# A PEER expert layer with 64 of 384 dense tokens moved to gathered rows, on one Trainium2 core

## The chip, the core and the metric

The kernel runs on one NeuronCore of a Trainium2 chip. TensorE (PE; its weight loads are shown as PEld), VectorE (DVE), ScalarE (ACT) and GpSimd (POOL) each work through a list of instructions in order and wait for each other on semaphores; SyncE (SP) and POOL issue the transfers between the core's memory (SBUF) and the device memory (DRAM), which 16 DMA engines carry out. The metric is the device time of one execution in microseconds (us), lower being better.

## The reference

512 tokens of width 1024 pass through one block: a modulated norm, a retention branch and a spatial gating branch, a residual, a second norm, and a PEER layer over 16,384 experts, each with one row of `expert_u` and one of `expert_v`. The change touches only the PEER layer:

```python
q = (hb @ w_q).reshape(T, PEER_HEADS, 2, PEER_HALF)
s = jnp.einsum('thpc,hpnc->thpn', q, sub_keys)
sub_s, sub_i = lax.top_k(s, K)                      # K = 16, 8 heads
...
expert = k1 * PEER_N_KEYS + k2                      # 8 x 16 = 128 experts for each token
g = jax.nn.softmax(top_s.astype(jnp.float32), axis=-1).astype(hb.dtype)
ue = expert_u[expert]
act = jax.nn.gelu(jnp.einsum('td,thkd->thk', hb, ue), approximate=False) * g
ve = expert_v[expert]
return jnp.einsum('thk,thkd->td', act, ve)
```

Behind it stand the second residual (`x + gate2 * peer`) and a final RMS norm.

## The kernel before

The first 500 us compute the two branches and the residual, and are not touched. The PEER layer handles its 512 tokens in two ways.

**Dense tokens** (`TA` = 384, token tiles 0 to 2, 128 tokens each) meet all 16,384 experts, in 128 chunks of 128 experts. For a chunk, `u_mm` multiplies a unit of `uT` (512 KB) with the normed tokens: 24 matmuls of 384 columns. Each float32 product is three passes over float32r parts: high by high, high by low, low by high. GELU follows, then a multiplication with a dense table of softmax weights (zero where a token has not chosen the expert); `a_make` does this (`aw` at L1235, rounded to `ah` at L1237, rest `al` at L1240). `v_mm` then takes each tile's 128 columns of `ah` or `al` as weights and a unit of `v` (its parts `wh`, `wl`) as the moving operand: 3 tiles x 3 passes x 2 halves of 512 columns, 18 matmuls for each chunk, all at L1252.

**Gathered tokens** (tile 3, 128 tokens, one on each partition) fetch only the rows they chose. `gather` (L1132) has POOL issue an indirect DMA of 128 rows of 4 KB, `consume` has DVE read it: a dot product with `h2B` (L1142) for a row of `u`, a weighted sum into `accB` (L1147) for a row of `v`. That makes 128 + 128 = 256 gathers.

The order is written out by hand. `plan()` sets the steps between the second norm and the main loop: the product keys and top-16 searches (`st1`, `st2`), the lists, the one-hot blocks (`oh`, then `wmm` on TensorE) which build the dense weight table, and beside them `U` steps, chunks of `u_mm` done ahead of the main loop, with their results written to DRAM (`sd`, L876, from `spl`). The planner adds 4.05 to its clock `P` for a `U` step and a cost to its clock `V` for each DVE step, lets DVE steps in while `V` is at most `P` + 6, and grants `GPU` = 0.75 `gather` steps for each `U`. It yields 78 `U` steps, 24 one-hot blocks of 16 tokens and 48 `gather` steps; 51 gathers are consumed before the main loop with the 3 left in their buffers. A finished pair of one-hot blocks goes to DRAM as 2 MB on POOL's queue (`wd`, L1118). In the one-hot part the gathers have three buffers, in the main loop eight.

The main loop (from L1371) runs over the 128 chunks; the last four are done tile by tile at the end. An iteration does `u_mm` two chunks ahead if that chunk was not done ahead of the loop, `v_mm`, the loads of `sd` and `wd` pieces on SP's queue, and `a_make`, with some `consume` and `gather` pairs put between `ah` and `al`; their number is spread evenly by `cost` and `per`. Units of `uT` and `v` come through `Stream`: a load on SP's queue five units ahead, a rounding on ACT to `wh` (L76), a subtraction on DVE to `wl` (L79).

After the loop `res` and `fin` (or `res_half`, `fin_half` for the last tile) add the residual and the final norm for one tile while TensorE does the next.

Of the kernel before, what the change touches and what calls it, by code (L numbers as in the profile page):

```python
# [17 lines left out]
OP = mybir.AluOpType  # L18
# [9 lines left out]
TA = 384  # L28
NA = TA // 128
# [6 lines left out]
GPU = 0.75  # L36
# [142 lines left out]
def block_kernel(ctx: ExitStack, tc: tile.TileContext, a, out, dbg=None):  # L179
# [28 lines left out]
    def rsqrt(p, dst, src, n, mul, tag):  # L208
        """dst = 1/sqrt(src*mul + EPS) with one Newton step."""
# [14 lines left out]
    # big and wt stay to the end; tmp serves the first half  # L224
# [23 lines left out]
    def ada_dma(k, where=None, eng=None):  # L248
        """unit k = [128 k, 8 kc, 256 cols] in two halves"""
# [6 lines left out]
    def ada_acc(k):  # L256
        """weighted sum over the k chunks, in two chains"""
# [14 lines left out]
    def ada_sum(acc, which, d, gcol):  # L272
        """shift and scale columns of channel chunk d; the gain is folded into the scale."""
# [98 lines left out]
    # x in, rms statistics; TensorE is kept busy meanwhile, for its clock  # L372
# [50 lines left out]
    # first pass: four token tiles of the first group and two of the second, by chunks of the contraction  # L423
    # as the modulation comes in
# [94 lines left out]
    # layer norm of the gated values  # L519
# [16 lines left out]
    # q, k with rotary, transposed to [dk, head, t]  # L536
# [28 lines left out]
    # spatial gating  # L565
# [47 lines left out]
    # gate b and the gated branch b, transposed  # L613
# [17 lines left out]
    # retention: P_h[j, i] = (k_j . q_i) * decay, unrolled over the key chunks  # L631
# [59 lines left out]
    # output gate of the retention branch, transposed with the group-norm gain  # L691
# [125 lines left out]
    def h2_split(t):  # L817
# [6 lines left out]
        if t == NA:  # L824
            for q in range(2):
# [3 lines left out]
                A.copy(h2B[:, q * 512:(q + 1) * 512], ps)  # L829
# [28 lines left out]
    def u_mm(parts=((0, TA),)):  # L858
# [619 lines left out]
```

## Time and profile before

| | us |
|---|---|
| median of 3 runs | 1778.95 (1775.25 to 1779.43) |
| span of the profiled execution | 1776.7 |
| TensorE busy in it | 1746.2 (98%) |
| VectorE busy | 1344.6 (76%) |
| ScalarE busy | 785.3 (44%) |
| GpSimd busy | 436.0 (25%) |

The profile is one execution; its span, first to last instruction, lies 2.3 us under the median of the runs. "Busy" of TensorE counts pipelined matmuls whose ends are modelled, so the distance between the starts of two matmuls tells more than the length of one. A "DMA share" is the mean busy share of the 16 DMA engines, and GB/s what they moved. The granted clock of TensorE is 1.0 at 2.4 GHz and 0.5 at 1.2 GHz.

### The profile page before, as it was taken

How to read it: one execution, taken by the hardware profiler on the slowest of the kernel's cores; microseconds unless marked ns; L12 is line 12 of the kernel's file. 1: busy time of each engine (PE TensorE's matmuls, PEld its weight loads, DVE VectorE, ACT ScalarE, POOL GpSimd, SP SyncE). 2: the span in 40 equal slices, each digit the busy share in tenths (PEclk: the TensorE clock that was granted, in tenths of full speed). 3: DMA queues.
4: the chain of work that ended last, by engine and by line, in shares of the span. 5: the costliest groups of instructions: out<-in, count | busy, mean ns of one | idle time of the engine just before them, and what ended most of it. 6: DMA issues, size and time to landing. Idle time of an engine off the chain costs nothing.

```text
span 1776.7 us, 24625 instructions
## 1 busy us (share of the span) xinstructions
PE 1746.2 (98%) x9117; PEld 1529.8 (86%) x9117; DVE 1344.6 (76%) x2618; ACT 785.3 (44%) x1051; POOL 436.0 (25%) x369
## 2 busy tenths in 40 slices
PE   9999999999999989999999999999999999999997
PEld 7888888888888889999999978888888888888885
DVE  7677762442754999999999767877778878878787
ACT  6532521333362344468999633333333333333334
POOL 0000100000010003233334233433434333434422
PEclk9999999999999999999999999999999999999998
DMA  9634742123433237777999999998989898989973
GB/s 379 228 106 147 260 178 83 60 95 107 143 119 116 72 102 268 267 250 242 337 329 331 341 380 342 339 339 323 333 324 348 326 338 331 342 306 356 338 274 132
DMA packets 119913, 445.47 MB, mean 251 GB/s; under 512 B 13360, under 2 KB 13360, under 8 KB 119664
## 3 DMA queue, kind: packets, MB, share of 16 engines
q1 hardware_dynamic: 67392, 246.61, 37.4%
q0 software_dynamic: 52400, 197.29, 31.8%
q8 instruction: 71, 1.16, 0.2%
q14 instruction: 50, 0.41, 0.1%
HBM read 399.15 MB, written 44.70 MB: 250 GB/s over the span
## 4 chain that ended last, share of the span: by engine, by line
PE 81%; DVE 10%; issue 4%; DMA 2%; POOL 1%; ACT 1%; SPq 0%; POOLq 0%; ACTq 0%; DVEq 0%
PE acc L1252 30%; PE mm L867 7%; PE mm L865 7%; PE mm L866 7%; PE mm L356 4%; PE mm L358 4%; PE mm L357 4%; PE mm L354 4%; PE mm L352 4%; PE mm L353 4%; DVE wl L79 2%; PE mm L1113 1%; PE mm L1114 1%; POOL gw L1132 1%; PE mm L668 1%
## 5 line engine op out<-in xcount | busy, mean ns | idle before, releaser
L79 DVE TENSOR_TENSOR wl<-raw,wh 128x1024 fp32r<-128x1024 f32 x356 | 436.0, 1228 | 257.7 <-ACT wh L76 256.9
L76 ACT CAST wh<-raw 128x1024 fp32r<-128x1024 f32 x356 | 373.2, 1052 | 84.4 <-PE mm L354 38.3
L867 PE MATMUL mm<-h2H,wl 128*128 128x384 f32 (+1 forms) x1032 | 346.9, 336 | 8.3 <-DVE wl L79 8.3
L865 PE MATMUL mm<-h2H,wh 128*128 128x384 f32 (+1 forms) x1032 | 348.3, 337 | 1.4 <-ACT wh L76 1.4
L866 PE MATMUL mm<-h2L,wh 128*128 128x384 f32 (+1 forms) x1032 | 345.5, 335 | 0.0
L1252 PE MATMUL acc<-wh,ah 128*128 128x512 f32 x768 | 244.4, 399 | 5.6 <-ACT ah L1237 5.6
L1252 PE MATMUL acc<-wl,ah 128*128 128x512 f32 x768 | 244.3, 399 | 0.0
L1252 PE MATMUL acc<-wh,al 128*128 128x512 f32 x768 | 244.0, 398 | 0.0
L1132 POOL DMA_INDIRECT gr<-in_v_dram,eidx x128 | 174.9, 1366 | 266.0 <-DVE wqb L1147 232.8
L1237 ACT CAST ah<-aw 128x384 fp32r<-128x384 f32 x128 | 65.8, 514 | 321.7 <-DVE aw L1235 321.7
L867 PEld LDWEIGHTS mm<-h2H,wl 128*128 128x128 f32 x1032 | 195.0, 189 | 11.4 <-DVE wl L79 11.3
L865 PEld LDWEIGHTS mm<-h2H,wh 128*128 128x128 f32 x1032 | 195.2, 189 | 4.2 <-ACT wh L76 2.0
L866 PEld LDWEIGHTS mm<-h2L,wh 128*128 128x128 f32 x1032 | 195.0, 189 | 1.9
L1252 PEld LDWEIGHTS acc<-wh,ah 128*128 128x128 f32 x768 | 145.0, 190 | 37.5 <-ACT ah L1237 6.4
L1252 PEld LDWEIGHTS acc<-wh,al 128*128 128x128 f32 x768 | 145.5, 189 | 35.8
L1252 PEld LDWEIGHTS acc<-wl,ah 128*128 128x128 f32 x768 | 145.5, 189 | 35.3
L1147 DVE SCALAR_TENSOR_TENSOR wqb<-gr,cB,wqb 128x1024 f32<-128x1024 f32 x128 | 164.1, 1282 | 1.9
L1132 POOL DMA_INDIRECT gr<-in_u_dram,eidx x77 | 99.5, 1292 | 160.1 <-DVE gr L1142 138.7
L352 PE MATMUL mm<-wh,hH 128*128 128x512 f32 x256 | 101.8, 398 | 0.0
L1132 POOL DMA_INDIRECT gw<-in_u_dram,eidx x51 | 75.5, 1480 | 102.0 <-DVE gw L1142 94.0
L354 PE MATMUL mm<-wh,hL 128*128 128x512 f32 x256 | 100.1, 391 | 0.2
L353 PE MATMUL mm<-wl,hH 128*128 128x512 f32 x256 | 99.8, 390 | 0.0
(292 smaller groups left out, 2745.9 us busy)
## 6 DMA issues: line engine op xcount, KB each, us to landing
raw<-in_uT_dram SPq DMA_DIRECT2D x128, 512.0 KB, 6.4
raw<-in_v_dram SPq DMA_DIRECT2D x128, 512.0 KB, 6.5
raw<-in_w_in_dram SPq DMA_DIRECT2D x60, 512.0 KB, 4.0
wqb<-wd SPq DMA_DIRECT2D x33, 768.0 KB, 9.3
wd<-stg POOLq DMA_DIRECT2D x12, 2048.0 KB, 12.5
sd<-spl POOLq DMA_DIRECT2D x39, 384.0 KB, 6.1
sp<-sd SPq DMA_DIRECT2D x39, 384.0 KB, 7.2
ada<-in_w_ada_dram POOLq DMA_DIRECT2D x28, 512.0 KB, 4.6
```

The lines of the kernel that those rows point to most:

```text
L76: self.nc.scalar.copy(h, r)
L79: self.nc.vector.tensor_tensor(l, r, h.bitcast(F32), op=OP.subtract)
L352: T.matmul(ps, sH[:, d, ab], wH[:, dd, :], start=st, stop=False)
L353: T.matmul(ps, sH[:, d, ab], wL[:, dd, :], start=False, stop=False)
L354: T.matmul(ps, sL[:, d, ab], wH[:, dd, :], start=False, stop=sp)
L356: T.matmul(ps, wH[:, dd, ab], sH[:, d, :], start=st, stop=False)
L865: T.matmul(ps[:, p:q], h[:, d, :], h2H[:, d, p:q], start=(d == 0), stop=False)
L866: T.matmul(ps[:, p:q], h[:, d, :], h2L[:, d, p:q], start=False, stop=False)
L867: T.matmul(ps[:, p:q], l[:, d, :], h2H[:, d, p:q], start=False, stop=(d == ND - 1))
L1132: P.indirect_dma_start(out=r, out_offset=None, in_=a["u"] if i < NJ else a["v"], in_offset=bass.IndirectOffsetOnAxis(ap=E_IDX[:, j:j + 1], ...
L1147: V.scalar_tensor_tensor(accB, r, cB[:, j:j + 1], accB, op0=OP.mult, op1=OP.add)
L1252: T.matmul(accs[2 * t + e], x[:, ts], y[:, e * 512:(e + 1) * 512], start=s0, stop=s1)
```

## The change

Half of tile 0 leaves the dense tokens: `TA` = 320. Its first 64 tokens (`HC` = 64) join the gathered ones. Each has 128 experts; the first 64 of them sit on partitions 0 to 63 and the other 64 on partitions 64 to 127 (`EC_IDX`, `gC`), so a gather again fills 128 partitions, and there are 64 + 64 = 128 more gathers of 512 KB. The two half sums are added at the end (`half_b`, `half_a`, `half_res`). Tile 0 has 64 dense tokens left; their 64 high and 64 low parts lie side by side in one tile (`hl`, from column `TA`), so one set of 128 weights carries both, and `v_mm` needs two passes instead of three for that tile: 16 matmuls for a chunk. The sum of the high and the low half comes out on different partitions and is added at the end too. `u_mm` and the table work on 320 columns, the one-hot blocks number 20. The planner's constants change, so its table does.

```diff
-TA = 384
-NA = TA // 128
+NA = 3
+TP = 128 * NA
+HC = 64
+TA = TP - HC
-GPU = 0.75
+GPU = 1.0
@@ plan
-        t["P"] += 4.05
+        t["P"] += 3.5
@@ u_mm
+                cs = slice(HC + p, HC + q)
+                T.matmul(ps[:, p:q], h[:, d, :], h2H[:, d, cs], start=(d == 0), stop=False)
...
@@ h2_split
-        if t == NA:
+        if t in (0, NA):
...
+                    P.dma_start(h2d[:, q * 512:(q + 1) * 512], hc[:HC, :])
@@ lists
+        if t == 0:
+            V.scalar_tensor_tensor(kc, kk[t][0][:HC], 128.0, kk[t][1][:HC], op0=OP.mult, op1=OP.add)
+            V.tensor_copy(ec, kc)
+            A.copy(EC_IDX[:HC, :], ec[:, :HJ])
+            P.dma_start(EC_IDX[HC:, :], ec[:, HJ:])
+            A.copy(gC[:HC, :], gA[:HC, 0:HJ])
+            P.dma_start(gC[HC:, :], gA[:HC, HJ:NJ])
@@ gather, consume
+    NGT = 2 * NJ + 2 * HJ
+    def seg(i):
+        if i < 2 * NJ:
+            return ("u", "v")[i // NJ], i % NJ, E_IDX, (h2B, dots, gB, accB, NJ)
+        i -= 2 * NJ
+        return ("u", "v")[i // HJ], i % HJ, EC_IDX, (h2C, dotC, gC, accC, HJ)
@@ a_make
-        h = mn.tile([128, TA], F32R, name="ah", tag="ah", bufs=4)
-        l = mn.tile([128, TA], F32R, name="al", tag="al", bufs=4)
+        hl = mn.tile([128, 2 * TA + HC], F32R, name="ah", tag="ah", bufs=4)
+        h, l = hl[:, 0:TA], hl[:, TA + HC:]
         A.copy(h, w)
+        A.copy(hl[:, TA:TA + HC], w[:, 0:HC])
@@ v_mm
+            if t == 0:
+                x = hl[:, TA:TA + 128]
+                runs = ((x, vh, st, False), (x, vl, False, sp))
+            else:
+                o = HC + (t - 1) * 128
+                h, l = hl[:, o:o + 128], hl[:, TA + HC + o:TA + HC + o + 128]
+                runs = ((h, vh, st, False), (h, vl, False, False), (l, vh, False, sp))
@@ the end
+    def half_b():
+        part = gr[1][:, 0:2, :]
+        P.dma_start(part[:HC, 1, :], accC[HC:, :])
+    def half_a():
+        for e in range(2):
+            A.copy(part[:, 0, HV[e]], accs[e])
+        nc.sync.dma_start(part[HC:, 1, :], part[:HC, 0, :])
+        A.copy(part[:HC, 0, :], accC[:HC, :])
+    def half_res():
+        V.tensor_tensor(part[:, 0, :], part[:, 0, :], part[:, 1, :], op=OP.add)
+        V.tensor_tensor(part[:, 0, :], part[:, 0, :], gates[:, 1, :], op=OP.mult)
+        V.tensor_tensor(x3[:, 0, :], x3[:, 0, :], part[:, 0, :], op=OP.add)
+        sq(0, slice(0, D), ss3[:, 0:1])
+        V.tensor_tensor(fo[:, 0, :], x3[:, 0, :], fo[:, NA, :], op=OP.mult)
+    half_b()
     for t in range(NA - 1):
         for i, vhl, hl in fin_l:
             v_mm(i, (t,), vhl, hl)
+        if t == 0:
+            half_a()
+            continue
         res(t)
         fin(t)
+        half_res()
+        fin(0)
```

What the planner's table becomes: 122 `U` steps instead of 78, 20 one-hot blocks instead of 24, 106 `gather` steps instead of 48 (55 ahead of the one-hot part, where 22 stood, and 51 in it, where 26 stood); with the last three buffers 109 gathers are consumed before the main loop, 275 remain for it. Of the chunks in the main loop 6 still do their `u_mm` there (50 before), four of these ahead of its first iteration.

TensorE, one chunk of the main loop, from its first matmul on (`acc` are the six banks, two for each token tile; `wh`, `wl` the unit of `v`). Before:

```order
L1252 MATMUL acc_9541<-wh,ah 128x512
L1252 MATMUL acc_9542<-wh,ah 128x512
L1252 MATMUL acc_9541<-wl,ah 128x512
L1252 MATMUL acc_9542<-wl,ah 128x512
L1252 MATMUL acc_9541<-wh,al 128x512
L1252 MATMUL acc_9542<-wh,al 128x512
L1252 MATMUL acc_9543<-wh,ah 128x512
```

And of the change (`ah` now holds both parts):

```order
L1299 MATMUL acc_10951<-wh,ah 128x512
L1299 MATMUL acc_10952<-wh,ah 128x512
L1299 MATMUL acc_10951<-wl,ah 128x512
L1299 MATMUL acc_10952<-wl,ah 128x512
L1299 MATMUL acc_10953<-wh,ah 128x512
```

The two matmuls with the low part as weights are gone for the first tile; the other two tiles keep six each.

VectorE in the main loop, two iterations in the middle (`wqb<-gr,cB,wqb` is a `consume` of a row of `v` into `accB`). Before:

```order
L1235 TENSOR_TENSOR aw<-sp_11932,wqb 128x384
L1147 SCALAR_TENSOR_TENSOR wqb<-gr,cB,wqb 128x1024
L1240 TENSOR_TENSOR al<-aw,ah 128x384
L79 TENSOR_TENSOR wl<-raw,wh 128x1024 x2
L1235 TENSOR_TENSOR aw<-gs,wqb 128x384
L1147 SCALAR_TENSOR_TENSOR wqb<-gr,cB,wqb 128x1024 x2
L1240 TENSOR_TENSOR al<-aw,ah 128x384
```

And of the change:

```order
L1274 TENSOR_TENSOR aw<-sp_11408,wqb 128x320
L1184 SCALAR_TENSOR_TENSOR wqb<-gr,dots,wqb 128x1024 x2
L1280 TENSOR_TENSOR ah<-aw,ah 128x320
L81 TENSOR_TENSOR wl<-raw,wh 128x1024
L1274 TENSOR_TENSOR aw<-sp_11408,wqb 128x320
L1184 SCALAR_TENSOR_TENSOR wqb<-gr,dots,wqb 128x1024 x3
L1280 TENSOR_TENSOR ah<-aw,ah 128x320
```

Two or three consumes stand in an iteration where one or two stood, and one `wl` in each, since `u_mm` has left the loop.

POOL in the one-hot part (`gw_` are the three gather buffers, by their numbers). Before:

```order
L1118 DMA wd<-stg 128x32x128
L876 DMA sd<-spl 128x768
L1132 DMA gw_6946<-in_u_dram,eidx 128x1024
L876 DMA sd<-spl 128x768
L1132 DMA gw_6944<-in_u_dram,eidx 128x1024
L1118 DMA wd<-stg 128x32x128
```

And of the change:

```order
L1145 DMA wd<-stg 128x32x128
L885 DMA sd<-spl 128x640
L1169 DMA gw_7939<-in_u_dram,eidx 128x1024
L1169 DMA gw_7940<-in_u_dram,eidx 128x1024
L885 DMA sd<-spl 128x640
L1169 DMA gw_7938<-in_u_dram,eidx 128x1024
L1169 DMA gw_7939<-in_u_dram,eidx 128x1024
L885 DMA sd<-spl 128x640
L1169 DMA gw_7940<-in_u_dram,eidx 128x1024
L1145 DMA wd<-stg 128x32x128
```

Between two writes of the table five gathers pass through the three buffers where two did.

## Rows read from the trace of the kernel before

**Rows 1.** The page: engines' busy time; then DMA share by 40 slices, in tenths.

```profile
PE 1746.2 (98%) x9117; PEld 1529.8 (86%) x9117; DVE 1344.6 (76%) x2618; ACT 785.3 (44%) x1051; POOL 436.0 (25%) x369
...
DMA  9634742123433237777999999998989898989973
```

**Rows 2.** The chain that ended last: start us, us, what; entry to the main loop.

```profile
1007.17 11.61 DMA wd<-stg
1019.00 7.80 DMA wqb<-wd
...
1028.05 15.41 PE acc L1252 x54
...
1060.27 12.65 PE acc L1252 x54
```

**Rows 3.** Stretches: us, PE, PEld, DVE, ACT, POOL busy (x), PEclk, DMA share, GB/s.

```profile
638.00:817.00 179.00, 170.93 (x967) 167.59 (x966) 171.10 (x620) 89.28 (x114) 51.57 (x50) 0.99 0.67 234
817.00:1004.00 187.00, 187.00 (x1590) 183.23 (x1589) 175.79 (x177) 174.85 (x185) 67.11 (x53) 1.00 0.96 325
...
1028.00:1746.00 718.00, 717.95 (x3339) 614.84 (x3340) 566.70 (x704) 249.37 (x343) 273.76 (x202) 1.00 0.90 332
...
1746.00:1776.00 30.00, 18.11 (x71) 13.90 (x69) 20.77 (x44) 13.76 (x24) 3.00 (x2) 0.86 0.18 70
```

**Rows 4.** Single matmuls of 256 and 384 columns in order of time: start us, us.

```profile
517.69 0.28 PE L866 MATMUL mm<-h2L,wh 128*128 128x256 f32 x1
517.81 0.28 PE L867 MATMUL mm<-h2H,wl 128*128 128x256 f32 x1
...
1207.31 0.34 PE L865 MATMUL mm<-h2H,wh 128*128 128x384 f32 x1
...
1211.47 0.39 PE L1252 MATMUL acc<-wh,ah 128*128 128x512 f32 x1
```

**Rows 5.** Groups of instructions, 817 to 1004 us: busy us, mean ns of one | idle before.

```profile
L865 PE MATMUL mm<-h2H,wh 128*128 128x384 f32 x274 | 93.6, 341 | 0.0
...
L1113 PE MATMUL mm<-ohA,ohB 128*128 128x128 f16 x384 | 45.8, 218 | 0.0
```

**Rows 6.** The same view, VectorE in the main loop, 1028 to 1746 us.

```profile
L79 DVE TENSOR_TENSOR wl<-raw,wh 128x1024 fp32r<-128x1024 f32 x171 | 211.1, 1235 | 146.8 <-ACT wh L76 146.8
...
L1147 DVE SCALAR_TENSOR_TENSOR wqb<-gr,cB,wqb 128x1024 f32<-128x1024 f32 x128 | 164.1, 1282 | 1.9
...
L1142 DVE SCALAR_TENSOR_TENSOR gr<-gr,h2B 128x1024 f32<-128x1024 f32 x77 | 91.6, 1220 | 0.0
L1240 DVE TENSOR_TENSOR al<-aw,ah 128x384 fp32r<-128x384 f32 x125 | 71.0, 568 | 2.4 <-ACT ah L1237 2.4
```

**Rows 7.** DMA issues of the whole span: number, size of each, median us to landing.

```profile
raw<-in_v_dram SPq DMA_DIRECT2D x128, 512.0 KB, 6.5
...
wqb<-wd SPq DMA_DIRECT2D x33, 768.0 KB, 9.3
...
sd<-spl POOLq DMA_DIRECT2D x39, 384.0 KB, 6.1
sp<-sd SPq DMA_DIRECT2D x39, 384.0 KB, 7.2
```

**Rows 8.** Stretches as in Rows 3, at the entry to the main loop.

```profile
1026.50:1051.50 25.00, 23.45 (x96) 19.59 (x97) 15.47 (x23) 8.51 (x13) 4.50 (x5) 0.86 1.02 410
...
1028.00:1033.00 5.00, 4.95 (x12) 3.88 (x13) 4.00 (x6) 2.15 (x4) 0.27 (x1) 0.50 1.02 412
```

**Rows 9.** DMA of the one-hot part, 817 to 1004 us: total, and two issues.

```profile
DMA packets 15650, 60.81 MB, mean 325 GB/s; under 512 B 1387, under 2 KB 1387, under 8 KB 15632
...
wd<-stg POOLq DMA_DIRECT2D x11, 2048.0 KB, 12.6
...
gw<-in_u_dram,eidx POOLq DMA_INDIRECT x25, 10.2
```

**Rows 10.** One full-width VectorE pass of `res` at the end: start us, us.

```profile
1759.66 1.23 DVE L1315 TENSOR_TENSOR fo<-x,fo 128x1024 f32<-128x1024 f32 x1
```

More of the change, by code (lines that the diff above doesn't have):

```diff
@@ L796, in block_kernel @@
     h2B = kp.tile([128, D], F32, name="h2B")
+    h2d = dr.tile([HC, D], F32, name="h2d")
     def h2_tile(t):
@@ L828, in h2_split @@
                     T.transpose(ps[:, i * 128:(i + 1) * 128], w[:, 4 * q + i, :], ident)
-                A.copy(h2B[:, q * 512:(q + 1) * 512], ps)
+                if t:
+                    A.copy(h2B[:, q * 512:(q + 1) * 512], ps)
+                else:
+                    hc = tmp2.tile([128, 512], F32, name="hc", tag="t2", bufs=5)
+                    A.copy(hc[:HC, :], ps[:HC, :])
+                    P.dma_start(h2d[:, q * 512:(q + 1) * 512], hc[:HC, :])
     x2_mm(0)
@@ L950, in block_kernel @@
     gB = kp.tile([128, NJ], F32, name="gB")
+    HJ = NJ // 2
+    EC_IDX = kp.tile([128, HJ], U32, name="ecidx")
+    gC = kp.tile([128, HJ], F32, name="gC")
     GX = None
@@ L1030, in lists_t @@
             T.transpose(ps[:, i * 128:(i + 1) * 128], w, ident)
-        ts = slice(t * 128, (t + 1) * 128)
+        f = 0 if t else HC
+        n = 128 - f
+        ts = slice(t * 128 + f - HC, (t + 1) * 128 - HC)
         o = 3584 + (t % 2) * 256
@@ L1126, in gather @@
         ng[0] += 1
-        if i >= 2 * NJ:
+        if i >= NGT:
             return
@@ L1212, in block_kernel @@
     wq_r = {f: wq_f[f][:, :8 * TA].rearrange("p (r b f t) -> p r b f t", r=2, b=NB, f=4) for f in (False, True)}
-    accB = wq_f[0][:, 8 * TA:8 * TA + D]
-    cB = mn.tile([128, NJ], F32, name="cB")
+    accB, accC = (wq_f[f][:, 8 * TA:8 * TA + D] for f in (False, True))
+    h2C = mn.tile([128, D], F32, name="h2C")
+    for f in (0, HC):
+        nc.sync.dma_start(h2C[f:f + HC, :], h2d)
     gr = [big([128, 4, D], F32, "gr") for _ in range(2)]
@@ L1240, in a_make @@
         V.tensor_tensor(l, w, h.bitcast(F32), op=OP.subtract)
-        at[c] = (h, l)
+        at[c] = hl
     accs = None
     def v_mm(i, tiles, vhl, hl, halves=(0, 1)):
-        (h, l), (vh, vl) = hl, vhl
+        vh, vl = vhl
         st, sp = (i == 0), (i == NCH - 1)
         for t in tiles:
-            ts = slice(t * 128, (t + 1) * 128)
-            for x, y, s0, s1 in ((h, vh, st, False), (h, vl, False, False), (l, vh, False, sp)):
+            if t == 0:
+                x = hl[:, TA:TA + 128]
+                runs = ((x, vh, st, False), (x, vl, False, sp))
+            else:
+                o = HC + (t - 1) * 128
+                h, l = hl[:, o:o + 128], hl[:, TA + HC + o:TA + HC + o + 128]
+                runs = ((h, vh, st, False), (h, vl, False, False), (l, vh, False, sp))
+            for x, y, s0, s1 in runs:
                 for e in halves:
-                    T.matmul(accs[2 * t + e], x[:, ts], y[:, e * 512:(e + 1) * 512], start=s0, stop=s1)
+                    T.matmul(accs[2 * t + e], x, y[:, e * 512:(e + 1) * 512], start=s0, stop=s1)
     V.memset(accB, 0.0)
+    V.memset(accB, 0.0)
+    V.memset(accC, 0.0)
     cap = [2.0]
@@ L1365, in block_kernel @@
     done = 0.0
-    left = 2 * NJ - ng[1]
+    left = NGT - ng[1]
     cost = [1 + (PRE <= i + LA and items[i + LA][1]) for i in range(NCH - LAST)]
@@ L1394, in block_kernel @@
         since += 1
-    assert since > 7
+    assert since > 7 and ng[1] == NGT
+    half_b()
     for t in range(NA - 1):
```

57 lines of the change are left out of this document (32 added, 25 removed).

## The prediction, made before the change was run

> **What bounds the kernel now.** I read the page first, for the busiest engine [rows 1]: TensorE works 98% of the span, VectorE 76%, and the DMA engines stand at 8 or 9 tenths in nearly every slice from the 22nd on. So there are two candidates for the second half, and the mean over the span hides where each of them rules. The table of stretches separates them [rows 3]. From 638 to 817 us TensorE, VectorE and DMA stand at 95%, 96% and 67%. In the one-hot part (817 to 1004 us) TensorE is at 100%, VectorE and ScalarE at 94%, DMA at 96%: all of them full at once. In the main loop TensorE is at 100% (717.95 of 718 us), VectorE at 79%, DMA at 90%. The chain of waits agrees: behind the last table write (11.6 us) and the first table load (7.8 us) it is matmuls of L1252 to the end [rows 2]. So TensorE is the bound of the loop, but DMA is only a tenth behind, and this change takes work from TensorE and gives 128 gathers of 512 KB, 67 MB, to DMA. The question is what the DMA engines can carry. Just after the loop's entry, while gathers and loads are both queued up, they carry 410 GB/s over 25 us at a share of 1.02 [rows 8]. That is the ceiling I use. At the loop's mean, 332 GB/s for a share of 0.90, a full share would be 369 [rows 3].
>
> **TensorE.** A matmul of 384 columns takes 4.16 us / 24 = 173 ns from start to start, one of 256 columns 120 ns [rows 4]; the slope is 0.417 ns a column, so 320 columns come to 147 ns, and a chunk of `u_mm` to 3.52 us for 4.16. The 512-column matmuls run at 12.65 / 54 = 234 ns [rows 2], so a chunk of `v_mm` goes from 18 (4.22 us) to 16 (3.75 us). A one-hot block costs what is left in its stretch: 274 / 8 = 34.25 chunks x 4.16 = 142.5 of 187 us, the other 44.5 over 24 blocks (384 / 16) is 1.85 us [rows 3, 5].
> Ahead of the loop, the part from the fourth `U` step on has 119 chunks where 75 stood: 418.9 for 312.0 us; four blocks fewer give 7.4 back. Sum +99.5 us. (The first three chunks save 2 us, the eight more transposes of tile 0 cost about as much.) The loop's 124 iterations fall from 718 us to 124 x 3.75 + 2 x 3.52 = 472, and the last four chunks by 1.9. On TensorE alone the kernel would end 148 us earlier, near 1629.
>
> **VectorE in the loop.** It is busy 566.7 us now [rows 3]. 275 gathers stand where 205 did: 64 more sums at 1.28 and 6 more dot products at 1.22 us are +89; 46 fewer `wl` at 1.235 us are -57; `al`, and `aw` which is like it, lose a sixth of 0.568 us each, 125 times, -24 [rows 6]. That gives 575 us, above TensorE's 472. ScalarE gets one more copy of 64 columns a chunk; at 249 of 718 us busy it hides that and loses 46 roundings. POOL gets 70 more gathers, a third more than it issues in its 274 busy us now, and stays far below.
>
> **DMA in the loop.** A unit is 512 KB = 0.524 MB, and so is a gather. 124 units of `v`, 2 of `uT` and 275 gathers are 210 MB; 31 table pieces of five sixths of 768 KB are 20.3; 61 pieces of `sd` of five sixths of 384 KB are 20.0 [rows 7]: 250.5 MB. (The same count of the kernel before, 375 units and gathers and its pieces, gives 236 MB; the profile moved 332 x 718 = 238.) At 410 GB/s these are 611 us, at 369 they are 679. So DMA becomes the bound of the loop, VectorE is 6% behind it and TensorE waits a quarter of the time. I take 630: 611, plus 6 for the first iterations, in which `RAMP` allows two to five gathers in flight where each iteration now wants 2.25, plus 13 (2%) because VectorE takes the rows in order and is nearly full itself. Eight gather buffers and five of `raw` keep both queues filled, which is why I stay near the ceiling. The gain of the loop is 718 - 630 = 88 us, and the stage ahead of it has cost 99.5.
>
> **DMA in the one-hot part.** Now 60.8 MB in 187 us, 11 of the transfers being table writes of 2.1 MB [rows 9]. The other 37.7 MB at 410 are 92 of the 0.96 x 187 = 179.5 us, so a write costs 8.0 us. With the change it has 55 chunks, 51 gathers, 10 writes: (51 + 55) x 0.524 + 27.5 x 0.328 = 64.6 MB, 157.5 us, and 80 for the writes, 237.5 us, beside 55 x 3.52 + 20 x 1.85 = 230.6 of TensorE. It is full, 7 us over. Then the three buffers: a gather each 4.5 us leaves a buffer 13.6 us, and its round is 10.2 to landing [rows 9], about 1.2 for the dot product [rows 6] and some 1.5 to issue, 13 in all. VectorE waits where one is late, and `wl` and the one-hots stand behind it. From nothing to 31 us (a landing of 12.6, as the writes have it, 17 rounds); I take 10, near the lower end since DMA is 3% over. In the stretch ahead of it DMA has room: 0.67 of share now, 55 gathers in it and four buffers.
>
> **Entry and end.** The entry stays: last block, table write, load, first weights, 24 us covered by five chunks, by 17.6 us of them now. The loop starts at 1028.05 + 99.5 + 10 = 1137.6, and its 124 iterations end at 1767.6. Behind 1746 stand 30.7 us now; 1.9 go. `half_res` and its norm stand on VectorE between tile 1 and the last tile: four passes of 1.23 us [rows 10] behind three of `res`, some 10 us with the small steps, beside 5.6 us of matmuls (24 x 234 ns), so the last tile's residual is about 5 us late. Span 1767.6 + 33.8 = 1801.4; the median of the runs lies 2.3 above the profiled span: **1803 us**, 1.4% slower.
>
> **Rivals.**
> A, faster: both queues stay filled through the loop. No debt in the one-hot part, 611 us, the end's 5 us hidden: 1127.6 + 611 + 28.8 + 2.3 = 1770. It decides from a mean of about 408 GB/s on. For it: 410 held for 25 us with both queues full [rows 8]. Against it: only 25 us of it are shown, behind a queue that had piled up, and VectorE is 94% full on that time. 0.19.
> B, TensorE's clock: in the loop TensorE waits some 1.3 us in each iteration. At the loop's entry, after it had waited for the first weights, 1028 to 1033 us ran at a granted clock of 0.50 (1.2 GHz), 12 matmuls in 5 us [rows 8], 0.41 us each. Half an iteration like that is 8 x 0.41 + 8 x 0.234 = 5.2 us, level with the loop's 5.1, so the clock can add some 0.2 us to each: +25, 1828. 0.10.
> C, the DMA engines go no better than the loop's mean and the three buffers hold up the one-hot part: 679 us and 20 more of debt, 1872. Half of both is 1840. 0.14.
> D, a lower limit of the memory. The Trainium skill ("DMA: Bandwidth & Descriptors", Where 436 GB/s comes from) says that between device memory and SBUF the memory's side binds, at about 358 GB/s for a core. By that figure the loop's 250.5 MB would be 700 us, an estimate from that page, and the time 1873. The trace speaks against it: 410 GB/s in [rows 8]. As a mechanism of this kernel it is C's end, a rate that falls back to 369 when the queues are long, and it is counted there with 0.03 more.
>
> **How the numbers follow.** Forecast, 1785 to 1825: 0.41. A, below 1773.6: 0.19. Between, within 0.3% (about what a measurement can tell from no change: 1773.6 to 1784.3): 0.13. B 0.10, C and D 0.17. So faster 0.19, same 0.13, slower 0.68. The range reaches down to 1765, A with five microseconds to spare, and up to 1865, short of C's far end: about 0.1 is left out on each side. The likeliest sign's own range is 1785 to 1865.
>
> **What would show it.** In the changed kernel's stretches the loop should start near 1138 us and last near 630 (5.1 us an iteration), with DMA at 0.97 or more of share and 390 to 410 GB/s, VectorE at 90% and TensorE at 75%; POOL's gathers should land later than 10 us after issue; waits of VectorE for gathered rows should appear, which are absent now. The part ahead should show a chunk of `u_mm` at 3.5 us, and DMA full from the first one-hot block to the entry. I am wrong if TensorE stays full in the loop (then DMA was no bound, and the end is far below 1765), if the part ahead grows by much less than 100 us, or if DMA stands below 0.9 with VectorE waiting: then it is latency, not rate.

## The result, and the profile after

The changed kernel takes 1844.83 us (median of 4 runs, 1843.94 to 1846.93), the kernel before 1779.19 on the same chip: a ratio of 1.0375, with a 95% interval of 1.0360 to 1.0389. It is **3.75% slower**, where 1.4% was forecast. The sign and the range (1765 to 1865) held, the size did not. The profiled execution spans 1845.2 us.

First the page of the changed kernel: busy time of TensorE and VectorE, then the DMA share by 40 slices in tenths and the rate in each (compare [rows 1]).

```profile
PE 1666.3 (90%) x8741; PEld 1421.3 (77%) x8741; DVE 1465.0 (79%) x2798; ACT 770.3 (42%) x1167; POOL 630.3 (34%) x522
...
DMA  9534742222441249988799998999999999999983
GB/s 378 213 111 142 275 156 79 80 81 91 160 150 58 81 158 353 350 318 294 266 332 335 353 340 324 381 357 408 408 408 408 408 393 409 408 405 408 407 349 124
```

TensorE is no longer at 98%. From the 28th slice to the 38th DMA stands at 9 with 408 GB/s nearly throughout: it looks as if one engine had taken the place of the other as the bound. The stretches of the changed kernel say the same by stage (us, PE, PEld, DVE, ACT, POOL busy with counts, granted clock, DMA share, GB/s; [rows 3] are the answer before):

```profile
642.00:836.00 194.00, 183.22 (x1214) 181.63 (x1214) 185.70 (x624) 83.69 (x117) 79.31 (x71) 0.97 0.82 289
836.00:909.00 73.00, 64.70 (x411) 62.77 (x410) 57.73 (x100) 38.67 (x55) 34.55 (x28) 0.95 0.86 294
909.00:1146.00 237.00, 224.49 (x1870) 219.74 (x1869) 203.91 (x226) 175.96 (x199) 109.75 (x84) 0.98 0.94 337
...
1179.00:1795.00 616.00, 512.39 (x1984) 385.88 (x1984) 575.28 (x724) 191.98 (x369) 359.77 (x271) 0.94 1.01 401
```

In the loop (last row) DMA is full, VectorE at 93%, TensorE at 83%. Ahead of it (the first three rows, the list part and then the one-hot part) TensorE idles 11, 8 and 13 us, and its granted clock is 0.97, 0.95 and 0.98; before, it was busy for 100% of the one-hot part at a clock of 1.00.

To compare kernels I read five marks off the matmuls in each trace: the start of the first `U` step behind the product keys, the start of the first and the end of the last one-hot matmul, the start of the first matmul of `v_mm` and, 124 iterations on, of the first of chunk 124. Between them lie the list part, the one-hot part, the entry and the loop. All in us; the time is the median of the runs (one run for e1, e3, e9, e12):

| kernel | first U | list part | one-hot part | entry | loop start | loop | time |
|---|---|---|---|---|---|---|---|
| before | 637.8 | 179.9 | 186.3 | 24.1 | 1028.1 | 717.5 | 1779.2 |
| after | 642.6 | 266.7 | 236.5 | 33.0 | 1178.9 | 631.8 | 1844.8 |
| e1_no_extra | 641.8 | 266.5 | 236.3 | 34.0 | 1178.5 | 474.4 | 1689.3 |
| e3_half_consume | 642.6 | 266.3 | 235.4 | 33.8 | 1178.2 | 619.8 | 1836.9 |
| e9_no_gather_oh | 641.6 | 265.8 | 218.4 | 23.1 | 1148.8 | 693.8 | 1881.9 |
| e12_none_ahead | 642.4 | 251.8 | 218.5 | 25.7 | 1138.4 | 769.0 | 1944.9 |
| e10_buf4g | 640.2 | 265.9 | 228.0 | 33.6 | 1167.6 | 624.1 | 1831.5 |
| e5_buf4 | 641.8 | 266.6 | 260.0 | 34.9 | 1203.3 | 624.4 | 1866.9 |
| e4_entry | 642.3 | 267.0 | 237.3 | 26.2 | 1172.8 | 632.0 | 1840.7 |
| e6_ecidx | 641.6 | 267.5 | 238.3 | 33.1 | 1180.5 | 627.8 | 1844.2 |
| e7_all | 640.9 | 266.3 | 260.2 | 27.8 | 1195.3 | 625.7 | 1861.9 |
| e8_gpu75 | 643.6 | 213.5 | 186.5 | 31.2 | 1074.8 | 709.8 | 1820.4 |
| e13_best50 | 640.7 | 184.6 | 161.3 | 26.4 | 1013.0 | 763.1 | 1814.1 |
| e14_gpu0 | 643.3 | 151.6 | 133.0 | 27.1 | 955.0 | 822.8 | 1813.7 |

Kernels whose stages are the same in code show what such a reading is worth: the list and one-hot parts agree within 2 us, the entry within 1, but the first `U` step lies anywhere from 640.2 to 643.6 and the loop varies from 624 to 632 (after, e4, e6, e10). A difference of a few us in the loop means nothing here.

So against the kernel before the loop gives back 85.7 us (88 forecast) and the end costs 3.4 more (3.1 forecast), but the loop starts 150.9 us later instead of 109.6. The 41 us that the forecast missed all lie ahead of the loop. Two questions follow: is the loop's bound really what I said, and where do the 41 us come from?

### The profile page after: what moved, and what is told of

Same layout as the page of the kernel before. It is cut to its first block, busy times and chain, and to the rows that moved or that the text cites. A ratio compares the mean times of both kernels' runs of the same rounds, so it can differ in the third digit from the quotient of the medians.

```text
span 1845.2 us, 24948 instructions
## 1 busy us (share of the span) xinstructions
PE 1666.3 (90%) x8741; PEld 1421.3 (77%) x8741; DVE 1465.0 (79%) x2798; ACT 770.3 (42%) x1167; POOL 630.3 (34%) x522
## 2 busy tenths in 40 slices
DMA packets 142702, 514.75 MB, mean 279 GB/s; under 512 B 16208, under 2 KB 16240, under 8 KB 142448
## 4 chain that ended last, share of the span: by engine, by line
PE 38%; DMA 22%; DVE 15%; issue 15%; POOL 7%; ACT 2%; SPq 0%; POOLq 0%; DVEq 0%; ACTq 0%
DMA gr<-in_v_dram,eidx 9%; DMA gr<-in_v_dram,ecidx 5%; PE mm L358 4%; PE mm L359 4%; PE mm L360 4%; POOL gr L1169 4%; DMA gr<-in_u_dram,ecidx 4%; PE mm L356 4%; PE mm L354 4%; PE mm L355 4%; DVE wl L81 3%; PE mm L876 3%; PE mm L874 3%; PE mm L875 3%; DMA gw<-in_u_dram,eidx 2%
## 5 line engine op out<-in xcount | busy, mean ns | idle before, releaser
L1299 PE MATMUL acc<-wh,ah 128*128 128x512 f32 x1280 | 407.3, 421 | 121.4 <-DVE ah L1280 121.1
L1299 PEld LDWEIGHTS acc<-wh,ah 128*128 128x128 f32 x1280 | 247.8, 200 | 215.5 <-issue 142.2
L876 PE MATMUL mm<-h2H,wl 128*128 128x320 f32 (+1 forms) x1032 | 326.5, 316 | 31.9 <-DVE wl L81 31.6
L874 PE MATMUL mm<-h2H,wh 128*128 128x320 f32 (+1 forms) x1032 | 326.8, 317 | 2.2 <-ACT wh L78 2.1
L875 PE MATMUL mm<-h2L,wh 128*128 128x320 f32 (+1 forms) x1032 | 324.1, 314 | 0.0
L1299 PE MATMUL acc<-wl,ah 128*128 128x512 f32 x768 | 257.7, 418 | 0.3 <-DVE wl L81 0.3
L1169 POOL DMA_INDIRECT gw<-in_u_dram,eidx x109 | 169.2, 1552 | 137.6 <-DVE gw L1179 118.0
L1299 PEld LDWEIGHTS acc<-wl,ah 128*128 128x128 f32 x768 | 154.9, 202 | 39.6 <-DVE wl L81 0.8
L1184 DVE SCALAR_TENSOR_TENSOR wqb<-gr,dots,wqb 128x1024 f32<-128x1024 f32 x128 | 164.1, 1282 | 17.8 <-DMA gr<-in_v_dram,eidx 16.2
L1179 DVE SCALAR_TENSOR_TENSOR gw<-gw,h2B 128x1024 f32<-128x1024 f32 x109 | 131.4, 1221 | 20.2 <-DMA gw<-in_u_dram,eidx 20.2
L1169 POOL DMA_INDIRECT gr<-in_v_dram,ecidx x64 | 88.5, 1383 | 54.9 <-DVE wqb L1184 36.8
L1169 POOL DMA_INDIRECT gr<-in_u_dram,ecidx x64 | 84.6, 1322 | 57.7 <-DVE gr L1179 37.9
```

Source lines behind the costliest of these rows:

```text
L874: T.matmul(ps[:, p:q], h[:, d, :], h2H[:, d, cs], start=(d == 0), stop=False)
L875: T.matmul(ps[:, p:q], h[:, d, :], h2L[:, d, cs], start=False, stop=False)
L876: T.matmul(ps[:, p:q], l[:, d, :], h2H[:, d, cs], start=False, stop=(d == ND - 1))
L1169: P.indirect_dma_start(out=r, out_offset=None, in_=a[tab], in_offset=bass.IndirectOffsetOnAxis(ap=ix[:, j:j + 1], axis=0))
L1179: V.scalar_tensor_tensor(r, r, 1.0, hx, op0=OP.mult, op1=OP.mult, accum_out=dt[:, j:j + 1])
L1184: V.scalar_tensor_tensor(acc, r, dt[:, j:j + 1], acc, op0=OP.mult, op1=OP.add)
```

## What bounds the loop: two experiments

The theory is that the loop's DMA volume at 400 to 410 GB/s sets it. The waits of the changed kernel from 1179 to 1795 us do not say so at first sight (engine and line, what it waited for, us in total, times, longest):

```profile
POOL gr L1169 <- DVE wqb L1184: 134.7, 98, 3.8
PE acc L1299 <- DVE ah L1280: 114.1, 90, 13.4
...
DVE wqb L1184 <- DMA gr<-in_v_dram,eidx: 16.2, 32, 1.2
POOL gr L1169 <- DMA gr<-in_v_dram,eidx: 15.3, 22, 2.2
```

TensorE waits 114 us, all for VectorE's low part of the weights, and VectorE itself waits for DMA only 16 us in this line. One could read VectorE as the bound. That is the rival, and it took two edits that pull the two apart.

**e1** keeps the dense half tile and leaves out the extra gathers:

```diff
-    NGT = 2 * NJ + 2 * HJ
+    NGT = 2 * NJ
```

> The changed kernel without the 128 gathers for the 64 moved tokens (their sums are left out, so their PEER output is missing); the dense half tile stays. Everything up to the loop is the same, so the loop should start near 1179 us. It then carries 147 gathers instead of 275, 183 MB instead of 250. Theory (the loop is bound by the DMA rate of about 408 GB/s): 449 us of DMA fall below TensorE's 472, TensorE becomes the bound again, the loop lasts 475 to 500 us at a DMA share near 0.95, and the kernel ends near 1695 to 1715 us. Rival (VectorE's order of work holds the loop: the low part of the weights comes late behind the rows): VectorE loses 164 us of sums but its chain in each iteration stays, TensorE keeps waiting for the low part, and the loop lasts 540 us or more.

The loop lasts 474.4 us, just under the 475 to 500 expected, and the kernel takes 1689.3, also just under its range. Its stages ahead of the loop last what the changed kernel's do (the table), so that this one run can be set beside it. The stretch of e1 (columns as above):

```profile
1179.00:1640.00 461.00, 461.00 (x1977) 371.65 (x1976) 424.84 (x534) 195.76 (x371) 163.86 (x142) 0.99 0.99 390
```

TensorE is full without a gap and its chain of waits is matmuls of L1299 for 98.6%. VectorE's order, with 92% of the stretch busy, does not hold TensorE. DMA stands at a share of 0.99 here too, with 390 GB/s, while TensorE has no gap: the share by itself does not name the bound. The kernel without the extra gathers ends at 1689 us, 89 us ahead of before. This also prices the gathers: 1844.8 - 1689.3 = 155.5 us for 128 of them, beyond everything that the dense half tile saves.

**e3** keeps every transfer and halves what VectorE reads of a gathered row in the loop:

```diff
-            V.scalar_tensor_tensor(acc, r, dt[:, j:j + 1], acc, op0=OP.mult, op1=OP.add)
+            V.scalar_tensor_tensor(acc[:, 0:512], r[:, 0:512], dt[:, j:j + 1], acc[:, 0:512], ...)
```

and in the same way the dot product.

> The changed kernel; in the main loop each gathered row is read over 512 of its 1024 columns only (half of the dot products and sums are left out there), while every gather still fetches its 4 KB rows. VectorE loses about 275 x 0.63 = 173 of its 575 us in the loop, DMA loses nothing. Theory (DMA rate): the loop stays at 612 to 632 us. Rival (VectorE, 94% full, is the bound or holds buffers back): the loop falls below 580 us, towards 500.

The loop lasts 619.8 us. The stretch of e3:

```profile
1179.00:1780.00 601.00, 497.31 (x1959) 384.27 (x1959) 424.38 (x715) 188.56 (x364) 280.02 (x270) 0.94 1.02 406
```

and two of its waits in the same window:

```profile
PE acc L1301 <- DVE ah L1282: 103.6, 53, 4.4
...
DVE wqb L1186 <- DMA gr<-in_v_dram,eidx: 84.4, 64, 2.5
```

VectorE fell to 71% of the stretch and the loop gained 12 us of 632, 2%. VectorE now waits 84.4 us in one line for the gathered rows of `v` (16.2 before the edit), and TensorE still waits 103.6 us for a VectorE that has a quarter of its time to spare. So DMA sets the loop. A nearly full VectorE costs at most those 12 us on top, which is what the forecast put there (13), though a loop of 624 us occurs with VectorE as full as ever (e10). The wait of TensorE for `ah` that the waits show in the changed kernel is only where the delay surfaces: VectorE takes its work in order, so the low part stands behind rows that DMA brought late, by a microsecond at a time. This last step is read from the order of the code and shown by no run: VectorE's own waits for rows add up to 33 us there, TensorE's for `ah` to 114.

## What makes the stage ahead late

TensorE's own work from the first `U` step behind the keys to the last one-hot matmul is 366.2 + 99.5 = 465.7 us by the forecast; with 10 of debt it expected 475.7. Measured are 503.3 (the list and one-hot parts together). In the one-hot part of the changed kernel, 909 to 1146 us, these waits are new:

```profile
DVE gw L1179 <- DMA gw<-in_u_dram,eidx: 19.7, 8, 3.6
ACT spl L883 <- DMA sd<-spl: 16.1, 7, 4.8
PEld mm L876 <- DVE wl L81: 14.3, 9, 3.1
PE mm L876 <- DVE wl L81: 11.8, 6, 2.9
```

and its chain of waits (start us, us, what) shows gathers as pieces of 12 and 14 us:

```profile
931.74 14.14 DMA gw<-in_u_dram,eidx
...
1008.34 12.42 DMA gw<-in_u_dram,eidx
```

VectorE waits for a row, `wl` stands behind it, TensorE waits for `wl`. To find how much of the lateness that is, two kernels keep the planner's table and drop gathers from it.

**e9** issues none in the one-hot part (59 stay ahead of the loop where 109 stood, so 50 go to it):

```diff
         elif k == "gather":
-            consume()
-            while ng[0] - ng[1] < len(gring):
+            if wx is None or ng[1] < ng[0]:
+                consume()
+            while wx is None and ng[0] - ng[1] < len(gring):
                 gather()
```

> The changed kernel with no new gathers issued in the one-hot part; those 51 go to the main loop. Theory (the stage ahead is late because its gathers share full DMA engines and three buffers): the time from the first U step behind the product keys to the last one-hot matmul, 503 us in the changed kernel, falls by 20 to 40 us to 465 to 483, and the waits of VectorE for gathered rows there (19.7 us) vanish. Rival (the lateness comes from the lists and from TensorE's clock, not from gathers): it falls by less than 10 us. In either case the loop gets 27 MB more, 66 us at 408 GB/s, and lasts 690 to 710 us.

**e12** issues none at all ahead of the loop:

```diff
         elif k == "gather":
-            consume()
-            while ng[0] - ng[1] < len(gring):
-                gather()
+            pass
```

and the four that `gstart` issues are gone too.

> The changed kernel with the same table but no gather issued ahead of the main loop: all 384 stand in it. Theory (what is left of the lateness with no gathers in the one-hot part, 484 us for a forecast of 466, comes from the 55 gathers that VectorE reads in the list part, where it is full): the time from the first U step behind the product keys to the last one-hot matmul falls to 464 to 470 us. Rival (it comes from the lists' new small steps and the clock): it stays at 480 to 484. In either case the loop gets 109 gathers more, 57 MB, 140 us: 765 to 785 us for 632.

Stretch of e9, its one-hot part:

```profile
909.00:1126.00 217.00, 216.17 (x1841) 213.38 (x1839) 150.10 (x129) 173.00 (x198) 28.92 (x34) 1.00 0.72 248
```

Stretch of e12, its list part and a little more:

```profile
642.00:909.00 267.00, 257.60 (x1764) 255.85 (x1763) 191.19 (x617) 133.93 (x184) 23.19 (x40) 0.98 0.55 183
```

And the loops of e9 and of e12:

```profile
1149.00:1820.00 671.00, 519.80 (x1957) 390.41 (x1958) 624.59 (x814) 188.64 (x363) 430.39 (x322) 0.92 1.02 406
...
1140.00:1890.00 750.00, 552.03 (x1982) 411.39 (x1980) 701.71 (x938) 190.29 (x367) 505.12 (x380) 0.89 1.02 405
```

In e9 TensorE is full in the one-hot part, which shrinks from 236.5 to 218.4 us: the 50 gathers cost **18 us** there. The whole stage takes 484.1 us, one more than the range that the theory gave. In e12 the list part shrinks too, from 266.7 to 251.8: the 55 gathers in it cost **15 us**. The stage takes 470.3, 0.3 above the expected range, and the forecast's 465.7 for TensorE alone was 4.6 short. The second cost is of another kind than the first. In the changed kernel VectorE is busy 185.7 of the 194 us from 642 to 836 and waits for a gathered row 0.5 us in all; it is simply full there, and 41 dot products at 1.22 us (50 us) are a good part of that. In e12 it has 191 of 267 us. The last 73 us (836 to 909) are less plain: VectorE has 79% there, and TensorE still idles 8.3 us, for `wl`, which in turn waits 14.9 us for ScalarE's rounding; without gathers TensorE idles 0.7 us in that window (e12). What links the two there was not taken apart. DMA also falls in e12, from 0.82 to 0.55 of share, but in the changed kernel those 0.5 us are the only wait for a transfer that any of the computing engines shows from 642 to 909 us.

Neither cost is waiting alone. By the rows, TensorE idles 12.5 us of the changed kernel's one-hot part and 0.8 of e9's, about 12 of the 18 us; for the rest its matmuls take longer, at a granted clock of 0.98 for 1.00. In the list part it idles 19.1 us (10.8 + 8.3) against 9.4 in e12, about 10 of the 15, at 0.97 and 0.95 for 0.98. Both loops took the displaced gathers at full rate (405 and 406 GB/s) and came out within the expected times.

**Are the three buffers or the full DMA engines the cause in the one-hot part?** My first form of the edit, **e5**, made room for a fourth buffer by halving a scratch tile of the one-hots:

```diff
-            gring = [wx.tile([128, D], F32, name="gw%d" % i) for i in range(3)]
+            gring = [wx.tile([128, D], F32, name="gw%d" % i) for i in range(4)]
@@ onehots, for each half y of the block
+            V.tensor_tensor(B_[:, y * HO:y * HO + HO, :], K2X.pop((b, y)), ..., op=OP.is_equal)
+            if y == 0:
+                k2_wide(b + 1, 1)
```

> The changed kernel with a fourth gather buffer in the one-hot part (paid for by a narrower scratch tile of the one-hots, made in two halves). Theory (three buffers hold VectorE up): the waits of VectorE for gathered rows from 909 to 1146 us fall from 19.7 us to under 5 and the loop starts 10 to 20 us earlier. Rival (DMA is full there, a buffer more only queues more): waits stay, loop start within 5 us, total within 5 us of 1844.8.

It became 22 us slower, and the waits tell why (e5, 909 to 1168.5 us):

```profile
DVE wl L81 <- ACT wh L78: 51.5, 18, 3.1
...
ACT k2x L1112 <- DVE ohB L1127: 47.4, 15, 5.1
...
PE mm L874 <- ACT wh L78: 20.8, 7, 3.8
```

The wait for gathered rows is gone (VectorE's line for the dot products shows 0.0 us of idle time), but ScalarE now reaches the copy of the second half before VectorE has freed its place, waits 47 us in all, and the roundings `wh` stand behind it. The experiment answered its question about the wait and nothing about the time, because it had brought a wait of its own. **e10** therefore takes the fourth buffer from the half of the gate tile that nobody reads any more:

```diff
-            gring = [wx.tile([128, D], F32, name="gw%d" % i) for i in range(3)]
+            gring = [wx.tile([128, D], F32, name="gw%d" % i) for i in range(3)] + [gates[:, 0, :]]
```

> The changed kernel with a fourth gather buffer in the one-hot part, this time in the half of the gate tile that has no reader after the first residual, so that the one-hots are untouched (in the earlier form of this edit ScalarE stood in order behind VectorE's halves of a one-hot, 47 us of wait that the edit itself brought). Theory (three buffers hold VectorE up): VectorE's waits for gathered rows from 909 to 1146 us go from 19.7 us to under 3, the time from the first U step behind the product keys to the last one-hot matmul goes from 503 to 485 to 495 us, total 1828 to 1838 us. Rival (DMA is full there, so a buffer only lengthens the queue): that time stays within 5 us of 503, the total within 5 us of 1844.8.

The time is 1831.54 us (ratio to before 1.0303, 1.0286 to 1.0320; the changed kernel's interval was 1.0360 to 1.0389). One wait and one stretch of e10, 909 to 1134 us:

```profile
DVE gw L1179 <- DMA gw<-in_u_dram,eidx: 5.8, 4, 2.1
```

```profile
909.00:1134.00 225.00, 216.38 (x1827) 211.77 (x1826) 200.55 (x222) 172.06 (x197) 107.55 (x82) 1.00 0.95 351
```

The wait falls from 19.7 to 5.8 us (under 3 was expected), the one-hot part from 236.5 to 228.0, halfway to the 218.4 without any gathers, and DMA moves 351 GB/s where it moved 337. The stage (list and one-hot parts) takes 493.9 us, inside the 485 to 495 expected. TensorE's idle time falls by 4 us (12.5 to 8.6), and the rest goes with a granted clock that is back at 1.00. So the want of a fourth buffer is half of that cost; the other half stays, with DMA at a share of 0.95 and VectorE at 89%, and no run separates these two. Part of the total's gain is an earlier first `U` step (2.4 us) and a loop of 624 us, both within their spread.

## What makes the entry late

The entry (last one-hot matmul to first `v_mm`) grew from 24.1 to 33.0 us. SP's queue in the changed kernel from 1146 us on:

```profile
1154.09 1.96 SPq L1253 DMA_DIRECT2D h2C<-h2d  x2
1156.15 3.98 SPq L60 DMA_DIRECT2D raw<-in_v_dram  x3
1160.22 0.46 SPq L60 DMA_DIRECT2D raw<-in_uT_dram  x1
1160.97 0.87 SPq L1262 DMA_DIRECT2D wqb<-wd  x2
```

its waits from 1130 to 1182 us, and one of ScalarE's from 1146 to 1179:

```profile
SPq L1253 <- DVE gw L1179: 13.1, 1, 13.1
...
ACT wh L78 <- DMA raw<-in_v_dram: 11.0, 2, 9.8
```

The load of the moved tokens' normed rows (`h2C`) goes into space that the gather buffers held. It waits for the last dot product and three units of `v` queue up behind it; they go out at 1156, share the engines with the first table load at 1160.97, and ScalarE waits 11.0 us for them before it can round `v` for the loop's first matmuls. **e4** issues that load in the eleventh iteration:

```diff
-    for f in (0, HC):
-        nc.sync.dma_start(h2C[f:f + HC, :], h2d)
...
         load_upto(i + LA + 2)
+        if i == 10:
+            for f in (0, HC):
+                nc.sync.dma_start(h2C[f:f + HC, :], h2d)
```

> The changed kernel with the load of the moved tokens' normed rows (two pieces on SP's queue) issued in the eleventh iteration of the loop instead of at the loop's entry. In the changed kernel SP waits 13.1 us there for the last gathers' buffers to be read, with the loads of v and of the table queued behind. Theory (this blocked queue costs the entry): the stretch from the last one-hot matmul to the first matmul of the loop falls from 33 to 24 us, total 7 to 10 us less than 1844.8. Rival (the table write of 12 us and the load behind it set the entry): less than 3 us.

The entry falls to 26.2 us, 6.8 of the 8.9 that had been added. The time is 1840.67 us (ratio 1.0349, 1.0332 to 1.0366), 4 us less, fewer than the 7 to 10 expected; the two intervals overlap, so that the profile's entry is the firmer number. The three units of `v` go out earlier in e4, from 1142.43 to 1152 us, though the table load is no earlier:

```profile
1142.43 9.59 SPq L60 DMA_DIRECT2D raw<-in_v_dram  x3
1159.54 0.33 SPq L60 DMA_DIRECT2D raw<-in_uT_dram  x1
1162.17 1.12 SPq L1260 DMA_DIRECT2D wqb<-wd  x2
```

e9 agrees: with no gathers in the one-hot part the same load of `h2C` goes out at 1118 us, before the last one-hot matmul, and the entry takes 23.1 us.

**e6** went after another new wait, at 820 us, where ScalarE's copy of the moved tokens' indices stands 6.7 us behind VectorE's index arithmetic:

```diff
-            A.copy(EC_IDX[:HC, :], ec[:, :HJ])
+            V.tensor_copy(EC_IDX[:HC, :], ec[:, :HJ])
...
-            A.copy(gC[:HC, :], gA[:HC, 0:HJ])
+            V.tensor_copy(gC[:HC, :], gA[:HC, 0:HJ])
```

> The changed kernel with the two small copies of the moved tokens' indices and weights on VectorE instead of ScalarE, so that ScalarE's roundings of uT do not stand behind VectorE's index arithmetic (6.7 us of ScalarE's wait at 820 us). Theory (that wait is part of the lateness): 2 to 4 us less. Rival (covered by the roundings done ahead): within 1 us.

Nothing: 1844.22 us, and the list part 267.5 for 266.7. The wait was there, is gone in e6, and cost nothing that shows. **e7** joined e4, e5 and e6:

> The three edits of the entry, of the fourth buffer and of the small copies together. Theory: the savings add, 20 to 30 us, 1815 to 1825 us, still slower than the kernel before at 1779. Rival: what one edit frees another resource takes back, total 1830 to 1840.

1861.93 us, outside both ranges. It carries e5's own wait, so the sum could not come out; against e5 it is 5.0 us better, with an entry of 27.8 for 34.9 us, which repeats the gain of e4.

## Where the gathers should stand

If DMA is full in the loop and VectorE in the list part, the only choice is where each gather costs less. Three kernels change the grant of gathers for each `U` step, and the planner's table follows it.

```diff
-GPU = 1.0
+GPU = 0.75
```

> The changed kernel with the old grant of 0.75 gathers for each U step. Its table then has 98 U steps instead of 122 and 60 gather steps instead of 106 (30 in the one-hot part instead of 51). TensorE loses 24 x 3.52 = 84 us ahead of the loop and the gather debt of the one-hot part should shrink by 15 to 25 us, so the loop starts near 1070 to 1080 us. The loop gets 46 gathers and 24 units of uT more, 33 MB net, 81 us of DMA, and VectorE 88 us more (663 us in all). Theory (DMA rate in the loop, DMA and buffers ahead of it): loop 710 to 725 us, total 1815 to 1835. Rival (the grant does not matter, the total is set by TensorE and DMA work that only moves): 1840 to 1850.

e13 has 0.5 (with the edits of e10 and e4), e14 has 0.0 (with those of e4 and e12).

> The changed kernel with a grant of 0.5 gathers for each U step, the fourth buffer as above, and the load of the moved tokens' rows taken out of the entry. Its table has 82 U steps and 33 gather steps; 46 units of uT and 347 gathers fall into the loop, 305 MB. Theory (DMA rate in the loop, TensorE ahead of it): loop start 985 to 1000 us, loop 760 to 775 us (748 by DMA at 408 GB/s, 765 of VectorE), total 1785 to 1810. Rival (VectorE and DMA both full cost each other 5% or more): 1820 or more.

> The changed kernel with no gathers granted ahead of the loop and the load of the moved tokens' rows taken out of the entry: 64 U steps ahead, 64 units of uT and all 384 gathers in the loop, 331 MB (810 us at 408 GB/s) and about 831 us of VectorE. Theory (ahead of the loop TensorE's work sets the time, in the loop the fullest of DMA and VectorE): loop start 915 to 930 us, loop 835 to 855, total 1785 to 1825. Rival (the stage ahead is held by VectorE's lists, not by TensorE): loop start 950 us or later, total 1830 or more.

The times are 1820.40 (ratio 1.0233, 1.0216 to 1.0250), 1814.12 (1.0199, 1.0182 to 1.0216) and 1813.71 us (1.0198, 1.0181 to 1.0215). The first step gains 24 us, the others hardly more (and e13 and e14 carry further edits, so that their 6 us are not the grant's alone), and none reaches the kernel before. Against what was expected: e8's total and start (1074.8) lie in their ranges, and its loop of 709.8 us just under 710. e13's loop of 763.1 us lies in its range, 15 above what 408 GB/s alone would give, and its start of 1013 misses 985 to 1000, so that the total misses its range as well. e14's loop of 822.8 us came in 12 under its range and its start at 955 for 915 to 930, which is what its rival said of the stage, though not of the total, which is in the theory's range. The rows of the three loops have 396, 392 and 394 GB/s. The stretches of e14 at the start of its list part and in its loop:

```profile
642.00:760.00 118.00, 106.69 (x688) 104.39 (x687) 112.17 (x524) 52.85 (x73) 8.20 (x16) 0.96 0.49 161
...
960.00:1790.00 830.00, 744.78 (x3446) 599.86 (x3445) 780.34 (x1017) 275.94 (x505) 526.83 (x381) 0.96 1.00 394
```

VectorE is full in the list part even with no gather in it, and in the loop DMA is full, VectorE at 94% and TensorE at 90%. With all three that full there is little left to move work into. The DMA total of the span says what the change costs in the end: 514.75 MB against 445.47 before; e1, without the extra gathers, moves 447.60.

## Why the prediction was right in sign and too small

**The bound of the loop: right.** DMA took over from TensorE; 631.8 us for a forecast of 630, with 396 GB/s over the whole loop, which is 250 MB for a forecast of 250.5. VectorE is busy 586 us for a forecast of 575 (the 575.28 further up are of 616 us only). e1 and e3 show the bound. The row of the whole loop:

```profile
1178.90:1810.70 631.80, 526.52 (x2033) 397.19 (x2034) 586.33 (x737) 198.49 (x382) 360.94 (x271) 0.94 1.00 396
```

The four lines of VectorE in the changed kernel's loop answer to [rows 6]:

```profile
L1184 DVE SCALAR_TENSOR_TENSOR wqb<-gr,dots,wqb 128x1024 f32<-128x1024 f32 x128 | 164.1, 1282 | 17.8 <-DMA gr<-in_v_dram,eidx 16.2
L81 DVE TENSOR_TENSOR wl<-raw,wh 128x1024 fp32r<-128x1024 f32 x122 | 148.6, 1218 | 4.2 <-ACT wh L78 4.2
L1184 DVE SCALAR_TENSOR_TENSOR wqb<-gr,dotC,wqb 128x1024 f32<-128x1024 f32 x64 | 84.7, 1323 | 7.4 <-DMA gr<-in_v_dram,ecidx 6.6
L1179 DVE SCALAR_TENSOR_TENSOR gr<-gr,h2C 128x1024 f32<-128x1024 f32 x64 | 76.5, 1220 | 10.1 <-DMA gr<-in_u_dram,ecidx 10.1
```

**TensorE's terms: right.** A chunk of `u_mm` and a block came out as forecast (in the one-hot part three chunks and one block take 12.41 us where nothing waits, 923.54 - 911.13, and 3 x 3.52 + 1.85 is 12.41), and e1's loop of 474.4 us is the 472 that TensorE alone was given.

**The stage ahead: the step that failed.** The forecast gave it TensorE's work, 10 us of debt and nothing else: the gathers of the list part and the longer entry were put at nothing, and the debt was taken too low. The missing 41.3 us (1178.9 - 1137.6) are, in order:
- 4.8 us at the first `U` step (642.6 for 637.8). That "the eight more transposes of tile 0 cost about as much" as three narrower chunks save was wrong by that: it counted their work and not their place. They stand at 504 us, where TensorE waits for ScalarE (L818); with tile 3's at 534 us that makes two waits of 4.4 us in all where one of 0.7 stood. Some of the rest is the clock: from 505 to 510 us it was granted at 0.66 behind that wait, while e10, with the same code and the same waits there, has 1.00 and is 2.4 us earlier at the first `U` step. The waits from 500 to 545 us, then this stretch of the changed kernel and of e10:

```profile
PE mm L831 <- ACT x L818: 4.4, 2, 2.9
...
505.00:510.00 5.00, 4.98 (x18) 4.00 (x18) 2.48 (x7) 3.03 (x7) 1.09 (x2) 0.66 0.11 34
...
505.00:510.00 5.00, 5.00 (x24) 4.14 (x23) 2.76 (x6) 2.71 (x5) 1.09 (x2) 1.00 0.17 38
```

- 14.9 us of the list part, where the 55 gathers were costed at nothing because "In the stretch ahead of it DMA has room". It had. VectorE had none (96% of 642 to 836 us), and the row that says so, 171 of 179 us [rows 3], was read in the first paragraph of the prediction and then not used. (e12)
- 18.1 us of the one-hot part for a debt of 10, whose bounds were 0 and 31. The mechanism was the one named: rows late in three buffers, `wl` behind them. Half of it goes with a fourth buffer. (e9, e10)
- 4.6 us of the stage that stay with no gathers in it (e12), not taken apart further.
- 8.9 us of the entry, of which "the entry stays" knew nothing. 6.8 of them are the added load on SP's queue, a DMA issue that stands in the changed code ahead of all loads of the loop. (e4)

Their sum, less the 10 already counted, is 41.3. With 1.8 more in the loop and 0.7 at the end that is the whole distance from the forecast span of 1801.4 us to the measured 1845.2.

**The rivals.** A did not come: 407 to 409 GB/s held in most slices, but the mean of the loop was 396 and its 632 us are 21 more than A's 611; above all the loop started 51 us later than in A. B is there in the row (granted clock 0.94 in the loop, and 0.89 in e12's loop) and costs nothing there that shows, since the loops of e3, e9 and e12 go by their bytes at 405 or 406 GB/s; where it does show is ahead of the loop, where TensorE sets the time and the forecast had not priced it. C's rate of 369 did not come, and its debt in the one-hot part came to 18 us for 30. That half of C, put at 1840 (half of its 69 us on 1803 is 1838), lies near the 1844.8 is luck, as most of C is rate. Nor did D's rate come: the Trainium skill ("DMA: Bandwidth & Descriptors", Where 436 GB/s comes from) has the memory's side bind at about 358 GB/s for a core; on this chip, with one core at work, the loop moved 401 over 616 us.

## What to carry to other kernels

Before work is moved from one engine to another, look at the receiving engine in every stage, not only in the one that the change is for: here DMA had a tenth to spare in the loop, and the change brought 67 MB at 408 GB/s, 164 us, to save 148 us of TensorE. A stage has as many bounds as it has full engines; room on one (DMA in the list part) says nothing of another that the same instruction passes through (VectorE). And a load that is added at a turn from one stage to the next stands ahead of all that follows on its queue: ask what frees its target, and issue it later if nobody needs it yet.

## What the runs showed of the hardware

The rate held: 401 to 406 GB/s at a share of 1.01 or 1.02 over 600 to 750 us (the changed kernel, e3, e9, e12), with gathers of 4 KB rows and plain loads mixed, where [rows 8] had shown 410 for 25 us. In the changed kernel's loop the median gather lands 14.7 to 15.1 us after issue (10.2 in the one-hot part before, [rows 9]) with no loss of rate; it has eight buffers there, and no run tried fewer.

Each transfer took longer while the rate rose: the median unit of `v` went from 6.5 us to landing [rows 7], in a loop at 332 GB/s, to 11.3 in one at 401.

TensorE's granted clock fell where it had waited: 0.98 in the changed kernel's one-hot part with 12.5 us of idle time, 1.00 in e9's with 0.8 and in e10's with 8.6.

GpSimd's issue of a gather of `v` takes 1232 ns at the median in the changed kernel's loop and 940 ns in e3's, where only VectorE's passes were cut to half their width. No run here separates the cause.
